# A hybrid decoder step on one core: projection stores on ScalarE's queue, the gate's low parts on GpSimd, constant products ahead of column sums

## The chip, the cores and the metric

The kernel runs on one core of a Trainium2 chip. The time is the device time in microseconds of one execution of the whole program; the profile is one such execution recorded by the hardware, on its own. TensorE (PE in the rows) makes the matrix products and writes to PSUM; VectorE (DVE), ScalarE (ACT) and GpSimd (POOL) do the rest on tiles of 128 partitions; SyncE (SP) issues most DMA transfers. Each engine works through its own instructions in order, and they wait for each other by semaphores.

## The reference, cut to what matters

One step of one layer of a decoder: 1024 prompt rows and 8 x 8 sample rows (1088 columns in the kernel, which works on the transposed activations), model width 1024.

```python
h = rms_norm(x, norm_mix_g)
proj = h @ w_in                       # 2*256 columns for a convolution branch, 3*768 for q, k, v
a = silu(layer_norm(depthwise_conv(a_val * sigmoid(a_gate)), ...))      # width 31
o = attend(q, k, v)                   # 12 heads of 64, three dilated windows, merged
x = x + concatenate([a, o]) @ w_out
h = rms_norm(x, norm_ffn_g)
g = depthwise_conv_valid(h @ w_ffn_gate)                                # width 3, 2816 channels
x = x + (silu(g) * (h @ w_ffn_up)) @ w_ffn_down
y = rms_norm(x, norm_final_g)
```

The outputs are y for prompt and sample, k and v for the caches, and the last rows of both convolutions. Everything is in float32.

## The kernel before

**Products in three parts.** A float32 product is made from two rounded parts of each operand: `hi` is the operand rounded to the type float32r (an ACT copy), `lo` is the remainder (operand minus `hi`, a subtraction on DVE or POOL). Three products (hi by hi, lo by hi, hi by lo) are added up in PSUM; lines 192 to 194 and 962 to 965 issue them. So each weight tile and each activation tile costs one ACT copy and one subtraction before TensorE can use it.

**Stages.** First the norm and the projections. `project(p)` (line 447) runs for six pairs of heads; each loads three weight tiles (q, k, v), makes the products, and DVE evicts them from PSUM into a tile `x`, 1088 columns wide, for each of the three (lines 469, 473). `prompt_part` (line 496) then splits q and k into high and low parts, and stores to memory what the attention will load again in another layout: the two parts of q into `dq` and of k into `dk` (line 505), k itself to its output (line 503), v to its output (line 507), and v transposed, by way of TensorE and two ACT copies, into `dv` (line 514). The first three projections go together with the sample rows' attention (`sample_attention`, cache tiles `cr`, line 176), the last three with the prompt's heads. `load_head` (line 617) loads `qs`, `kk`, `vf` and `vw` back. `scores` and `weighted` do the prompt's attention: masked scores on TensorE and DVE, exponentials on ACT (line 718), transposes on TensorE (line 745), their copies on ACT or DVE, and the products with v (line 766).

**The output projection** comes in three parts of 3, 3 and 2 tiles of 128 input channels (PARTS), because it starts before the last heads are done. The last part (from line 941) works on two halves of 544 columns. Its inputs and weights are loaded by a chain of loads on SP's queue (`queued`, `load_input`); `parts_of` (line 1011) splits a weight or an input, with ACT for the high part and POOL for the low part. Among the loads are the first tiles of the feed-forward gate, `gate_raw` (line 1067): four tiles 128x512, whose high parts ACT makes at line 1083 and whose low parts DVE makes at line 1084. The gate's first products (`two_products`, line 981, output px) read them.

`out_half(h, hook)` (line 1174) goes over the eight output tiles of a half in a fixed order. For each it makes the products into a pair of PSUM banks (`pair`, four pairs in rotation), DVE adds them to the residual (line 1188), ACT squares the sum (line 1197) and DVE adds up the squares (line 1201). In the second half the first three tiles also have a deferred product with the middle part's inputs; after that product of the second tile (j = 1) the hook `norm_first` (line 1214) puts the column sums of the first half's squares: `root` (line 207), five products with a column of ones (line 214), and a short chain on DVE and ACT that ends in the inverse root. `spread` (line 232) turns that into a row for all partitions, after j = 2.

**What sets the order.** A planner simulates the program and writes each engine's order by it; `tc.issue_after(x)` pins an instruction behind x, and where nothing pins it the planner chooses. DMA issues are instructions of the engine whose queue they are on, so a transfer that waits for its data holds up what stands behind it on that engine. `load_w` (line 155) already makes its low parts on POOL in pieces 256 wide (`cut`). `onesc` (line 141) is a constant 128x128 tile; a few products of it with itself stand at the kernel's start (line 296) and among its first products (line 362).

Of the kernel before, what the change touches and what calls it, by code (L numbers as in the profile page):

```python
# [18 lines left out]
F32 = mybir.dt.float32  # L19
# [5 lines left out]
P = 128  # L25
D = 1024
# [45 lines left out]
HF = NF // 2  # L72
BEHIND = 3
GS = (6, 7)
PO = 240
GW = 2 + S + B * (T + 2)
HALF = ((0, HN // 2), (HN // 2, HN // 2))
# [9 lines left out]
def trunk_kernel(tc, xT, w_in, w_first, w_out, w_gate, w_up, w_down, par, kc, vc, sa, sf, pmask, smask,  # L87
                 yT, kT, vT, ca, cas, cf):
    nc = tc.nc
    with (  # L90
# [50 lines left out]
        onesc = cp.tile([P, P], F32, name="onesc")  # L141
# [65 lines left out]
        def root(sq, div, width):  # L207


            ps = bank(*rbank[0])  # L210
            size = sizes(width)
            nt = len(size)
            for i, n in enumerate(size):
                summed[0] = nc.tensor.matmul(ps[:n, i:i + 1], sq[:, i * P:i * P + n], ones, start=True, stop=True).ins
            v = sp.tile([P, 9], F32, tag="rv", name=nm("rv"), bufs=2)[:, :nt]
            nc.vector.memset(v, 1.0)
            nf = width // P
            nc.vector.tensor_scalar(v[:, 0:nf], ps[:, 0:nf], 1.0 / div, EPS, op0=ALU.mult, op1=ALU.add)
            if nf < nt:
                n = size[-1]  # L220
                nc.vector.tensor_scalar(v[:n, nf:nt], ps[:n, nf:nt], 1.0 / div, EPS, op0=ALU.mult, op1=ALU.add)
            r = sp.tile([P, 9], F32, tag="rr", name=nm("rr"), bufs=2)[:, :nt]
            nc.vector.reciprocal(r, v)
            squared[0] = nc.scalar.activation(r, r, AF.Sqrt).ins

            t = sp.tile([P, 9], F32, tag="rt", name=nm("rt"), bufs=2)[:, :nt]
            nc.vector.tensor_mul(t, r, r)
            nc.vector.scalar_tensor_tensor(t, t, -0.5, v, op0=ALU.mult, op1=ALU.mult)
            rooted[0] = nc.vector.scalar_tensor_tensor(r, t, 1.5, r, op0=ALU.add, op1=ALU.mult).ins
            return r  # L230
# [63 lines left out]
        ps = bank("S", "g", 3)  # L294
# [152 lines left out]
        def project(p, pump):  # L447
            W = [load_w(w_in[4 + 6 * c + p], KT, nc.gpsimd, cut=2 * P) for c in range(3)]
            dq = dp.tile([2, P, S], F32, name=nm("dq"))
            dk = dp.tile([2, P, S], F32, name=nm("dk"))  # L450
            dv = dp.tile([S, P], F32, name=nm("dv"))
            if p < NS1:
                new, vn = zt("S", "new", 2, "new", 2 * NS), zt("S", "vn", 2, "vn", P)
            else:
                new, vn = zt("P", "new", NP - NS1, "new", 2 * NS), zt("P", "vn", NP - NS1, "vn", P)
            nc.gpsimd.memset(vn[NS:, :], 0.0)
            spill[p] = (dq, dk, dv), new, vn
            xs = {}

            evicted = [None]  # L460

            def product(c):
                if c not in xs:
                    xs[c] = keep("qkv")
                x = xs[c]

                def ev(ps, t0, n):
                    m = min(n, S - t0)
                    nc.vector.tensor_mul(by_class(x)[:, t0 // 4:(t0 + m) // 4, :],
                                         ps[:, :m].rearrange("p (j c) -> p j c", c=4),  # L470
                                         R[:, t0:t0 + m].rearrange("p (j c) -> p j c", c=4))
                    if m < n:
                        evicted[0] = nc.vector.tensor_mul(x[:, S:N], ps[:, m:n], R[:, S:N]).ins  # L473

                last = p == NP - 1 and c == 2
                gemm(W[c], h, KT, ev, ([("A", "g", GA)] * GA + [("A", "r", 1)]) if last else None)

            def split_qk(c, hi, lo, cols):
                x = xs[c][:, cols]
                if c == 0:  # L480
                    nc.scalar.activation(hi, x, AF.Copy, scale=-0.125)
                    nc.vector.scalar_tensor_tensor(lo, x, -0.125, hi.bitcast(F32), op0=ALU.mult, op1=ALU.subtract)
                else:
                    nc.scalar.activation(hi, x, AF.Copy)
                    nc.vector.tensor_sub(lo, x, hi.bitcast(F32))

            def sample_part(c):
                if c < 2:
                    nc.scalar.activation(new[:, c * NS:(c + 1) * NS], xs[c][:, S:N], AF.Copy,
                                         scale=(1.0 if c else -0.125))  # L490
                else:
                    pt = bank(*gbank[0])
                    nc.tensor.transpose(pt[:NS, :P], xs[c][:, S:N], ident)
                    nc.scalar.activation(vn[:NS, :], pt[:NS, :P], AF.Copy)

            def prompt_part(c):
                x = xs[c]
                if c < 2:
                    hi, lo = zbig("qkh", F32R, S), zbig("qkl", F32R, S)
                    split_qk(c, hi, lo, slice(0, S))  # L500
                if c < 2:
                    if c:
                        nc.sync.dma_start(kT[p * P:(p + 1) * P, :], x)
                    for part, t in ((0, hi), (1, lo)):
                        nc.sync.dma_start((dq, dk)[c][part], t.bitcast(F32))
                else:
                    nc.sync.dma_start(vT[p * P:(p + 1) * P, :], x)
                    vs = zbig("vs", F32, S)
                    for i0 in (0, 4):
                        pt = bank(*gbank[0])  # L510
                        for i in range(4):
                            nc.tensor.transpose(pt[:, i * P:(i + 1) * P], x[:, (i0 + i) * P:(i0 + i + 1) * P], ident)
                        nc.scalar.activation(vs[:, i0 * P:(i0 + 4) * P], pt, AF.Copy)
                    nc.sync.dma_start(dv.rearrange("(t p) d -> p t d", p=P), vs.rearrange("p (t d) -> p t d", d=P))

            for c in range(3):
                product(c)
                if c == 2 and p < NS1:
                    with tc.issue_after(evicted[0]):
                        pump(STEPS[c])  # L520
                else:
                    pump(STEPS[c])
                sample_part(c)
                prompt_part(c)
# [390 lines left out]
        part = load_part(PARTS[0], staged, g_part)  # L915
# [27 lines left out]
        def pair(s="g", tag="g2"):  # L943

            return zone[pairs[0] + "ps"].tile([P, 1024], F32, tag=tag, name=nm(s), bufs=pairs[1])
# [65 lines left out]
        def parts_of(raw, hi, lo):  # L1011

            done = nc.scalar.activation(hi, raw, AF.Copy).ins
            nc.gpsimd.tensor_sub(lo, raw, hi.bitcast(F32))
            return done

        part, late_lows = [[], []], []
# [25 lines left out]
        for h, tag in enumerate(("b11", "t2")):  # L1043
# [4 lines left out]
            for m0 in ORDER[h * 4:h * 4 + 4:2]:  # L1048
                raw = slot("b11", "wr", F32, 2 * n * P)
                queued(raw.rearrange("p (m c) -> p m c", m=2), w_out[m0:m0 + 2, :, k0 * P:].rearrange("m p c -> p m c"))  # L1050
                hi, lo = early["b21"].pop() if early["b21"] else slot("b21", "wh", w=512), slot("b21" if m0 == ORDER[0] else "t3", "wl", w=512)
                with tc.issue_after(last_high):
                    last_high = parts_of(raw, hi, lo)
                hi, lo = [t.rearrange("p (k c) -> p k c", c=P) for t in (hi, lo)]
                for j in range(2):
                    wl[m0 + j] = hi[:, j * n:j * n + n], lo[:, j * n:j * n + n]
        for i in range(n1):
            lo, hi = slot("b21", "ml"), slot("t3", "mh")
            raw = lo.bitcast(F32)
# [12 lines left out]
        for m in ORDER[:DEFER]:  # L1072
            hi, lo = [slot("b22", t, w=n1 * P) for t in ("wh", "wl")]
# [7 lines left out]
        for r, (hi, lo) in zip(gate_raw, tiles):  # L1081
            with tc.issue_after(last_high):
                last_high = nc.scalar.activation(hi, r, AF.Copy).ins
            nc.vector.tensor_sub(lo, r, hi.bitcast(F32))

        blocks = {tag: [None] * 4 for tag in BTAGS}
        made, high = [], [None]
# [77 lines left out]
        raw = [slot("t2", "wr", F32, half) for _ in range(4)]  # L1165
# [45 lines left out]
        sq0, _ = out_half(0, None)  # L1211
        rs = []

        def norm_first(j, last):
            if j == 1:
                with tc.issue_after(last):
                    rs.append(root(sq0, D, HN))
                order = squared[0]
                for x, (hi, lo) in up_parts:
                    with tc.issue_after(order):  # L1220
                        order = nc.scalar.activation(hi, x, AF.Copy).ins
                    with tc.issue_after(rooted[0]):
                        nc.vector.tensor_sub(lo, x, hi.bitcast(F32))
            elif j == 2:
                with tc.issue_after(last):
                    rs[0] = spread(rs[0], new_root, HN)
# [301 lines left out]
        w, act = [], []  # L1528
# [45 lines left out]
        for k, (g, unit) in enumerate(UNITS):  # L1574
# [16 lines left out]
            for i, product in enumerate(unit):  # L1591
                b, key, outs = product
                for m in range(4):
# [6 lines left out]
                    for r, h in outs:  # L1600
                        x = x2[4 * r + m][:, h * HN:h * HN + HN]
# [67 lines left out]
        for i, (t0, n) in enumerate(TAIL):  # L1669
            r = []  # L1670
# [20 lines left out]
        v, r, t = [sp.tile([P, 9], F32, tag=tag, name=nm(tag), bufs=2)[:, :nt] for tag in ("rv", "rr", "rt")]  # L1691
# [118 lines left out]
```

## Time and profile before

| | us |
|---|---|
| median of 3 runs | 1316.93 |
| lowest and highest | 1312.14, 1317.67 |
| the profiled execution | 1320.17 |
| its span, first to last instruction | 1318.4 |
| mean granted TensorE clock | 0.993 of full |
| TensorE busy | 1293.7 |
| VectorE busy | 932.1 |
| ScalarE busy | 561.2 |
| GpSimd busy | 503.0 |

Rows of the profile are quoted below word for word. In a group's row stand line, engine, operation, output<-inputs and count, then busy time and mean; in a row of time, start and length in us come first and the idle time before, with what ended it, last in brackets. In a row of waits stand the engine and line that waited, what it waited for, and total us, count and longest. In a row of windows stand the stretch, its length, and busy us (with the number of instructions) of PE, PE's weight loads, DVE, ACT and POOL, then the granted TensorE clock, the mean busy share of the 16 DMA engines, and GB/s. "SPq" is SP's instruction queue. A matmul's length in a row includes the time through the array; successive starts show the pace.

### The profile page before, as it was taken

What the parts mean: (1) busy time and instruction counts of PE and PEld (TensorE: products, weight loads), DVE (VectorE), ACT (ScalarE), POOL (GpSimd) and SP (SyncE); (2) the same over time, 40 slices, a digit from 0 to 9 for tenths busy, and PEclk for the clock granted to TensorE, in tenths of its full rate; (3) what the DMA queues carried; (4) which work ended last, traced back from release to release, by engine and by line L of the source; (5) the groups of instructions that cost most, each with busy time, mean ns of one, the idle gap of its engine ahead of it and who ended that gap; (6) DMA issues with size and microseconds to landing.
All of it is one profiled execution on the core that took longest, in us unless ns stands there. A gap on an engine that the chain in (4) does not pass through costs nothing.

```text
span 1318.4 us, 26089 instructions
## 1 busy us (share of the span) xinstructions
PE 1293.7 (98%) x10336; PEld 1252.6 (95%) x10336; DVE 932.1 (71%) x1788; ACT 561.2 (43%) x1124; POOL 503.0 (38%) x475
## 2 busy tenths in 40 slices
PE   9999999999999999899999999999999999999997
PEld 8999999999978889899999999999999999999997
DVE  7478879555674657589976767667776569868656
ACT  7312121547684564455433323333233344334523
POOL 0242223211111117321765645656465535444611
PEclk9999999999999999999999999999999999999998
DMA  9248778565789987360213323133312395352413
GB/s 320 65 151 294 270 255 217 158 174 139 235 271 293 289 272 207 102 228 18 75 50 124 124 92 110 47 124 109 108 65 91 113 358 188 109 185 90 158 36 102
DMA packets 93530, 211.43 MB, mean 160 GB/s; under 512 B 13792, under 2 KB 42592, under 8 KB 93408
## 3 DMA queue, kind: packets, MB, share of 16 engines
q1 hardware_dynamic: 92688, 208.89, 48.2%
q8 instruction: 81, 1.33, 0.4%
q10 hardware_dynamic: 720, 0.88, 0.2%
q14 instruction: 41, 0.34, 0.1%
HBM read 153.69 MB, written 56.04 MB: 159 GB/s over the span
## 4 chain that ended last, share of the span: by engine, by line
PE 79%; DVE 12%; DMA 5%; issue 2%; ACT 1%; SPq 0%; POOL 0%; DVEq 0%; ACTq 0%
PE g L192 6%; PE g L193 6%; PE g L194 6%; PE py L962 5%; PE py L964 5%; PE py L965 4%; PE g L962 4%; PE g L965 4%; PE g L964 4%; PE pz L964 3%; PE pz L965 3%; PE pz L962 3%; PE o L766 3%; PE px L962 3%; PE px L965 3%; PE px L964 3%
## 5 line engine op out<-in xcount | busy, mean ns | idle before, releaser
L167 POOL TENSOR_TENSOR wl<-wr,wh 128x256 fp32r<-128x256 f32 x96 | 85.3, 918 | 253.6 <-PE g L194 111.0
L192 PE MATMUL g<-xh,wh 128*128 128x384 f32 (+1 forms) x472 | 156.9, 332 | 0.3 <-DVE qkv L473 0.2
L194 PE MATMUL g<-xh,wl 128*128 128x384 f32 (+1 forms) x472 | 155.5, 330 | 0.0
L193 PE MATMUL g<-xl,wh 128*128 128x384 f32 (+1 forms) x472 | 155.1, 329 | 0.0
L962 PE MATMUL g<-ux,as 128*128 128x272 f32 x504 | 145.1, 288 | 0.4 <-DVE x L1602 0.4
L965 PE MATMUL g<-ux,as 128*128 128x272 f32 x504 | 145.3, 288 | 0.0
L964 PE MATMUL g<-ux,as 128*128 128x272 f32 x504 | 144.7, 287 | 0.0
L1116 POOL TENSOR_TENSOR wb<-wr,wb 128x512 fp32r<-128x512 f32 x79 | 115.6, 1475 | 50.7 <-ACT wb L1115 50.7
L1512 POOL TENSOR_TENSOR as<-ar,as 128x640 fp32r<-128x640 f32 (+1 forms) x56 | 90.4, 1625 | 103.2 <-ACT as L1511 91.4
L1115 ACT ACTIVATE wb<-wr 128x512 fp32r<-128x512 f32 x79 | 49.7, 629 | 163.5 <-DVE wr L1150 104.3
L1116 POOL TENSOR_TENSOR wa<-wr,wa 128x512 fp32r<-128x512 f32 x40 | 63.7, 1593 | 91.3 <-ACT wa L1115 85.3
L962 PEld LDWEIGHTS g<-ux,as 128*128 128x128 f32 x504 | 95.0, 189 | 0.8 <-issue 0.8
L718 ACT ACTIVATE y<-y,m 128x128 f32<-128x128 f32 (+1 forms) x192 | 88.5, 463 | 16.6 <-DVE m L706 13.1
L965 PEld LDWEIGHTS g<-ux,as 128*128 128x128 f32 x504 | 94.8, 188 | 0.0
L964 PEld LDWEIGHTS g<-ux,as 128*128 128x128 f32 x504 | 94.6, 188 | 0.0
L1380 DVE SCALAR_TENSOR_TENSOR fc<-gb,prm,fc 128x1104 f32<-128x1104 f32 x44 | 82.0, 1885 | 14.7 <-ACT fc L1378 14.4
L192 PEld LDWEIGHTS g<-xh,wh 128*128 128x128 f32 x472 | 88.7, 188 | 2.1 <-issue 0.6
L193 PEld LDWEIGHTS g<-xl,wh 128*128 128x128 f32 x472 | 88.8, 188 | 0.3
L194 PEld LDWEIGHTS g<-xh,wl 128*128 128x128 f32 x472 | 88.8, 188 | 0.0
L681 DVE CUSTOM_DVE_ANT_0 y<-s,pmk 128x128 f32<-128x128 f32 (+1 forms) x192 | 63.6, 376 | 27.6 <-PE s L677 25.4
L419 DVE SCALAR_TENSOR_TENSOR cacc<-gp,prm,cacc 128x1024 f32<-128x1024 f32 x60 | 79.8, 1329 | 0.1
L163 ACT ACTIVATE wh<-wr 128x1024 fp32r<-128x1024 f32 (+1 forms) x28 | 28.0, 999 | 111.5 <-PE g L194 93.2
(413 smaller groups left out, 4309.2 us busy)
## 6 DMA issues: line engine op xcount, KB each, us to landing
cr<-in_kc SPq DMA_DIRECT2D x24, 768.0 KB, 8.5
cr<-in_vc SPq DMA_DIRECT2D x24, 768.0 KB, 7.7
ux<-ub SPq DMA_DIRECT2D x63, 272.0 KB, 4.1
kk<-dk SPq DMA_DIRECT2D x48, 256.0 KB, 6.2
wr<-in_w_in SPq DMA_DIRECT2D x20, 512.0 KB, 5.2
wr<-in_w_gate SPq DMA_DIRECT2D x20, 512.0 KB, 3.2
wr<-in_w_up SPq DMA_DIRECT2D x20, 512.0 KB, 4.5
ub<-u SPq DMA_DIRECT2D x18, 544.0 KB, 3.4
```

The lines of the kernel that those rows point to most:

```text
L167: lo_eng.tensor_sub(lo[:, t], raw[:, t], hi.bitcast(F32)[:, t])
L192: nc.tensor.matmul(ps[c], whi[:, k, :], xh[:, t0:t0 + n], start=(k == 0), stop=False)
L193: nc.tensor.matmul(ps[c], whi[:, k, :], xl[:, t0:t0 + n], start=False, stop=False)
L194: nc.tensor.matmul(ps[c], wlo[:, k, :], xh[:, t0:t0 + n], start=False, stop=(k == nk - 1))
L419: eng.scalar_tensor_tensor(acc[:, :S], gp[:, j:j + S], col(w0 + j), acc[:, :S], op0=ALU.mult, op1=ALU.add)
L718: nc.scalar.activation(y, y, AF.Exp, bias=m[:, 4 * g + i:4 * g + i + 1], scale=-1.0, accum_out=den[:, g, 2 * hd + u, i:i + 1])
L962: nc.tensor.matmul(ps, whi[:, k, :], xh[:, t], start=(start and k == 0), stop=False, skip_group_check=True)
L964: nc.tensor.matmul(ps, whi[:, k, :], xl[:, t], start=False, stop=False, skip_group_check=True)
L965: last = nc.tensor.matmul(ps, wlo[:, k, :], xh[:, t], start=False, stop=(stop and k == nk - 1), skip_group_check=True).ins
L1116: nc.gpsimd.tensor_sub(lo, x, hi.bitcast(F32))
L1380: nc.vector.scalar_tensor_tensor(c[:, :W], gb[i][:, t:t + W], col(C_FW + 3 * f + t), c[:, :W], op0=ALU.mult, op1=ALU.add)
L1512: nc.gpsimd.tensor_sub(lo, raw, hi.bitcast(F32))
```

## The change

Three edits. In `prompt_part` the stores of k's output, of both high parts, of v's output and of `dv` are issued from ACT's queue; the low parts stay on SP's. In the output projection's last part the subtractions of `parts_of` are cut into two halves of the width, and the gate's low parts go from DVE to POOL, also in two halves. In `norm_first` three products of `onesc` with itself, into a pair of PSUM banks of their own whose content nothing reads, are put between the deferred product of j = 1 and the column sums, which are pinned behind them.

```diff
+BRIDGE = 3
...
                 if c < 2:
                     if c:
-                        nc.sync.dma_start(kT[p * P:(p + 1) * P, :], x)
-                    for part, t in ((0, hi), (1, lo)):
-                        nc.sync.dma_start((dq, dk)[c][part], t.bitcast(F32))
+                        nc.scalar.dma_start(kT[p * P:(p + 1) * P, :], x)
+                    for part, t, store in ((0, hi, nc.scalar.dma_start), (1, lo, nc.sync.dma_start)):
+                        store((dq, dk)[c][part], t.bitcast(F32))
                 else:
-                    nc.sync.dma_start(vT[p * P:(p + 1) * P, :], x)
+                    nc.scalar.dma_start(vT[p * P:(p + 1) * P, :], x)
...
-                    nc.sync.dma_start(dv.rearrange("(t p) d -> p t d", p=P), vs.rearrange("p (t d) -> p t d", d=P))
+                    nc.scalar.dma_start(dv.rearrange("(t p) d -> p t d", p=P), vs.rearrange("p (t d) -> p t d", d=P))
...
         def parts_of(raw, hi, lo):
 
             done = nc.scalar.activation(hi, raw, AF.Copy).ins
-            nc.gpsimd.tensor_sub(lo, raw, hi.bitcast(F32))
+            w = raw.shape[-1] // 2
+            for t in (slice(0, w), slice(w, 2 * w)):
+                nc.gpsimd.tensor_sub(lo[:, t], raw[:, t], hi.bitcast(F32)[:, t])
             return done
...
                 last_high = nc.scalar.activation(hi, r, AF.Copy).ins
-            nc.vector.tensor_sub(lo, r, hi.bitcast(F32))
+            for t in (slice(0, D // 4), slice(D // 4, D // 2)):
+                nc.gpsimd.tensor_sub(lo[:, t], r[:, t], hi.bitcast(F32)[:, t])
...
             if j == 1:
                 with tc.issue_after(last):
+                    ps = pair()
+                    for _ in range(BRIDGE):
+                        end = nc.tensor.matmul(ps[:, :P], onesc, onesc, start=True, stop=True).ins
+                with tc.issue_after(end):
                     rs.append(root(sq0, D, HN))
```

## The prediction

> **What bounds the kernel now.** I read the page's head first, then the waits of TensorE, then the windows of 20 us, and last the order of time around the two places that the change touches.
>
> ```profile
> span 1318.4 us, 26089 instructions
> PE 1293.7 (98%) x10336; PEld 1252.6 (95%) x10336; DVE 932.1 (71%) x1788; ACT 561.2 (43%) x1124; POOL 503.0 (38%) x475
> PE o L766 <- DMA vw<-dv: 2.9, 1, 2.9
> PE g L214 <- DVE sq L1201: 1.0, 1, 1.0
> 380.00:400.00 20.00, 18.34 (x146) 14.23 (x144) 15.42 (x51) 14.54 (x45) 0.87 (x1) 1.00 1.03 348
> 400.00:420.00 20.00, 17.14 (x143) 16.00 (x145) 9.63 (x41) 9.46 (x27) 2.44 (x5) 0.91 0.97 285
> 580.00:600.00 20.00, 19.91 (x153) 19.48 (x153) 19.00 (x31) 11.64 (x21) 0.00 (x0) 0.98 0.26 99
> ```
>
> The reader sees that TensorE (PE) sets the end: it stands idle for 1318.4 - 1293.7 = 24.7 us of the whole span, 1.9%. No change that leaves the products alone can win more than that and the stretches at a lower granted clock (the third column from the right, 0.91 and 0.98 above). Two idle places belong to this change. One is a wait for the load of vw at about 408 to 411 us, behind the projections. The other is a wait of the column sums (L214) for the running sum of squares, in the output projection's last part. I take the second first, since it can be worked out.
>
> **The output projection's last part.** These are VectorE's (DVE) and TensorE's rows in order of time, with two of GpSimd's (POOL).
>
> ```profile
> 559.29 4.02 POOL L1014 TENSOR_TENSOR ml<-ml,mh 128x544 fp32r<-128x544 f32 x3
> 566.21 4.14 POOL L1014 TENSOR_TENSOR wl<-wr,wh 128x384 fp32r<-128x384 f32 x3 [2.90 <-DMA wr<-in_w_up]
> ...
> 562.78 1.11 DVE L1201 TENSOR_TENSOR sq<-sq,sq 128x544 f32<-128x544 f32 x1
> 569.40 1.55 DVE L1201 TENSOR_TENSOR sq<-sq,sq 128x544 f32<-128x544 f32 x1
> 570.86 0.71 DVE L1188 TENSOR_TENSOR x<-g,x 128x544 f32<-128x544 f32 x1
> 571.50 0.71 DVE L1201 TENSOR_TENSOR sq<-sq,sq 128x544 f32<-128x544 f32 x1
> 572.13 1.28 DVE L1084 TENSOR_TENSOR wa<-wr,wa 128x512 fp32r<-128x512 f32 x2
> 573.33 1.28 DVE L1084 TENSOR_TENSOR wb<-wr,wb 128x512 fp32r<-128x512 f32 x2
> 574.54 0.71 DVE L1201 TENSOR_TENSOR sq<-sq,sq 128x544 f32<-128x544 f32 x1
> 575.17 0.71 DVE L1188 TENSOR_TENSOR x<-g,x 128x544 f32<-128x544 f32 x1
> 575.81 0.71 DVE L1201 TENSOR_TENSOR sq<-sq,sq 128x544 f32<-128x544 f32 x1
> ...
> 575.39 0.28 PE L965 MATMUL g<-mh,wl 128*128 128x272 f32 x1
> 576.66 1.22 PE L214 MATMUL g<-ones,sq 128*128 128x1 f32 x10 [0.99 <-DVE sq L1201]
> 577.82 0.59 PE L962 MATMUL g<-mh,wh 128*128 128x272 f32 x1
> 580.93 0.32 PE L964 MATMUL g<-ml,wh 128*128 128x272 f32 x1
> ```
>
> The four subtractions of L1084 (the gate's low parts) hold VectorE from 572.13 to 574.54, 2.4 us, ahead of the last two additions of squares. TensorE ends its products at 575.39 + 0.28 = 575.67 and waits 0.99 us. What follows is slower too: 13 products start between 577.82 and 580.93, 0.239 us apart.
>
> ```profile
> 578.00:578.50 0.50, 0.50 (x3) 0.50 (x4) 0.33 (x3) 0.10 (x1) 0.00 (x0) 0.50 0.15 57
> 574.13 0.29 PE L964 MATMUL g<-ml,wh 128*128 128x272 f32 x1
> ```
>
> The granted clock is 0.50 there. At the full clock ten such products lie between 574.13 and 575.39, 0.126 us apart, so the 13 would take 1.64 us and not 3.11: 1.47 us lost. The place costs 0.99 + 1.47 = 2.46 us.
>
> What the change puts there. The subtractions become eight on GpSimd, half as wide (128x256). The nearest rows for one, and for one constant product of the bridge (two records each), are these:
>
> ```profile
> L167 POOL TENSOR_TENSOR wl<-wr,wh x96: 723/739/1854, 46.3 to 536.2; 128x256 fp32r<-128x256 f32 x96
> L362 PEld LDWEIGHTS g<-onesc x6: 188/192/192, 5.7 to 6.4; 128*128 128x128 f32 x6
> ```
>
> Eight by 0.74 is 5.9 us of GpSimd after 570.35, to 576.3, or some 577.5 with the halved L1014 before them and VectorE's operations in between. Nothing wants them before the gate's first product:
>
> ```profile
> 591.73 0.13 PE px L983
> ```
>
> That is 14 us later, so the work is hidden; without this cover its cost would be at most those 5.9 us.
>
> But GpSimd's work holds up VectorE's additions. The one at 562.78 ended at 563.89, 0.58 after GpSimd's run ended (559.29 + 4.02 = 563.31). The one at 569.40 ended at 570.95, 0.60 after GpSimd's end at 570.35. So an addition of two SBUF tiles seems to wait out the GpSimd operation under way; the additions from PSUM (L1188) keep their 0.71. With the subtractions gone, VectorE needs four steps (three L1201, one L1188) from 571.50, 0.63 apart, so it is done at 574.0; with a whole 0.74 of waiting before each of the three, at 576.2. The bridge is six records some (6.4 - 5.7)/5 = 0.14 us apart, 0.84 us: TensorE is through it at 575.67 + 0.84 = 576.51. Both ends of VectorE's range lie before that. The sums then start at 576.51 and not 576.66: 0.15 us won, and if TensorE isn't idle the 1.47 us of half clock go as well. The term is **-1.6 us**; its ends are -2.5 (no bridge cost at all) and +0.84 (bridge paid, nothing won). After that the same chain runs on behind TensorE's order, so what is won is kept: VectorE, 19.00 of 20 us busy from 580 to 600, starts that stretch from the root that these sums feed.
>
> The Trainium skill ("TensorE: Matmul & The Clock Gate", Part 1) says that the clock falls after an idle window of about 3.4 us, and that the windows run freely. This trace shows the fall after 0.99 us of waiting and 1.2 us of one-column sums, so the idle need not last a window. By the rule the half clock would stay where the windows happen to lie badly, and the term would be -0.15 us.
>
> The halves of parts_of. Each halved operation costs GpSimd 2 x 0.74 in place of one 128x512 row.
>
> ```profile
> 554.30 5.04 POOL L1014 TENSOR_TENSOR wl<-wr,wh 128x512 fp32r<-128x512 f32 x4
> L896 POOL TENSOR_TENSOR x<-x,xr x32: 752/769/1040, 500.4 to 528.7; 128x272 f32<-128x272 f32 x32
> 555.84 0.36 PE L962 MATMUL g<-mh,wh 128*128 128x272 f32 x1 [0.75 <-DVE x L900]
> ```
>
> 5.04/4 = 1.26 becomes 1.48; 4.02/3 = 1.34 becomes 2 x 0.77 = 1.54; the 128x384 stay between 1.38 and 1.48. The first seven add 1.5 us, inside the 2.90 us that GpSimd waits before 566.21. The first of the last three would end by 567.7, where TensorE (96 products from 555.84 at 0.126) wants it near 568. I take +0.1 us, ends 0 and +0.6.
>
> **The projections' stores.** Per projection seven stores; five (k's output, both high parts, v's output, dv) go to ScalarE's (ACT) queue, 30 in all, and the two low parts stay. These are SyncE's queue (SP) waits from 60 to 365 us, then its order behind the last projection:
>
> ```profile
> SPq L507 <- DVE qkv L473: 31.9, 5, 8.5
> SPq L503 <- DVE qkv L473: 29.7, 5, 11.9
> PE ss L596 <- DMA cr<-in_vc: 0.8, 2, 0.4
> PE s L677 <- DMA qs<-dq: 0.6, 1, 0.6
> ...
> 370.28 0.34 SPq L507 DMA_DIRECT2D out_vT<-qkv  x1
> 373.39 0.54 SPq L159 DMA_DIRECT2D wr<-in_w_out  x1
> 376.06 0.38 SPq L514 DMA_DIRECT2D dv<-vs  x1
> 376.49 2.26 SPq L281 DMA_DIRECT2D mx<-mixed  x3
> SPq L176 <- PE t L745: 2.3, 1, 2.3
> ```
>
> The long waits of the queue before 365 us cost TensorE almost nothing: the loads behind them make it wait 0.8 + 0.6 us. Behind the last projection dv holds the queue from 373.93 to 376.49, 2.56 us, and the loads of mx, of the caches, of qs, kk, vf and vw follow in order. Without it they could go up to 2.5 us earlier. Two things take from that: the queue's own 2.3 us wait for TensorE among the cache loads, and the DMA engines, which are full (shares 1.03 and 0.97 in the first windows). So vw lands between 0 and 2.5 us earlier, out of the 2.9 us wait. I take 1.0, nearer to the low end because of the full engines; no clock is counted.
>
> ScalarE pays 30 x 0.34 = 10.2 us for issuing, the length of the L507 row. Most lies in its idle time (43% busy). Behind a store that waits on VectorE stand the exponentials (L718), the copies of the transposed weights (L751) and the weights' high parts (L163), and TensorE's transposes and products wait for those. SyncE's queue loses the 30 issues; GpSimd's issues nothing. Ends: 0, and 10.2 if each stood on the path; I take +0.3.
>
> **Sum.** -1.6 + 0.1 - 1.0 + 0.3 = -2.2 us. The profiled execution took 1320.17 us, 1.8 around its span, so it would become 1318.0. The median of the runs is 1316.93, 3.2 lower; the same difference gives **1314.7 us**.
>
> **Rivals.**
> 1. The vw wait goes wholly, with its half clock: the 2.9, some 1.7 lost to the 0.91 (0.09 x 20), the 1.4 of the other loads, and the 1.6 above, less 0.4: 7.2 us, 1309.7. For it: the queue waits are long. Against it: full DMA engines.
> 2. The stores' move does nothing, because the same bytes go through the same full engines. Then -1.6 + 0.1 + 0.3 = -1.2: 1315.7. For it speak shares of 1.03 and 0.97 just ahead of the vw wait. The Trainium skill ("DMA: Bandwidth & Descriptors", Issuing engines are not separate DMA queues) says the same: only issue time is saved.
> 3. The bridge is not covered, or the planner puts the sums ahead of the second product's rest, before VectorE is ready: TensorE still waits and the clock still falls. Up to 0.84 is paid and nothing won there: 0.84 + 0.1 - 1.0 + 0.3 = +0.2, 1317.2.
> 4. Slower: ScalarE stands at the stores. In SyncE's queue the same stores stood up to 11.9 us. If ScalarE's order puts one ahead of exponentials whose transposes TensorE wants, TensorE waits and falls to half clock. At some 3 us and 1.5 us of clock a time, two of the six projections give +9 beside the -1.6 + 0.1 of the other part: 1324.4. It decides from the point where the store's wait exceeds the slack of the exponentials, which are at most 0.7 us late now.
>
> ```profile
> PE t L745 <- ACT y L718: 1.1, 2, 0.7
> ```
>
> **How the numbers follow.** Chances: forecast 0.42, rival 1 0.14, rival 2 0.22, rival 3 0.14, rival 4 0.08. The order that the planner writes may also shift elsewhere by a microsecond or two either way; so rivals 2 and 3 and the forecast are read with some 2 us around them. The range 1307.5 to 1321 takes in all but rival 4 and the far end of rival 1. A change under 0.5% (6.6 us) is about what can't be told from none here: below 1310.3 lies most of rival 1 and a little of the forecast, 0.15; above 1323.5 rival 4, 0.08; between, 0.77.
>
> **What would show it.** Right: L214 in that part without a wait, granted clock 1.00 from 576 to 581, the gate's low parts on GpSimd before 580; the vw wait near 2 us. Wrong: a half clock still there; L745 or L766 waiting on ScalarE by more than now; cache loads later, not earlier. A change of TensorE's order in the projections would make the sum void.

## The result, and the profile after

| | before | after |
|---|---|---|
| median, us | 1315.46 (4 runs) | 1337.52 (4 runs) |
| lowest to highest | 1312.14 to 1317.67 | 1336.06 to 1338.52 |
| the profiled execution | 1320.17 | 1336.72 |
| its span | 1318.4 | 1334.9 |

The changed kernel takes 1.0146 times as long, with an interval of 1.0111 to 1.018. The forecast was 1314.7 us and the range ended at 1321.0. Run again later, beside other experiments (e8 below), it took 1.0088 times as long, 1.0059 to 1.0116: slower both times, but not by the same amount.

These are TensorE's longest waits in the changed kernel (total us, count, longest). Numbers of lines after 74 are higher by 1, by up to 4 in the last part.

```profile
PE s L678 <- DMA qs<-dq: 5.2, 2, 4.1
PE o L767 <- DMA vw<-dv: 4.1, 1, 4.1
PE s L656 <- DVE xe L653: 4.1, 3, 3.4
```

The wait for vw was to become shorter than its 2.9 us; it is 4.1, and the one for qs stands above it. The wait of the column sums is gone from the list. Where the time went is seen by following three marks that both kernels have: the last copy of vs behind the projections, the first product of the output projection's last part (555.84 before) and the end. First the copy in the kernel before, then both marks in the changed one:

```profile
375.44 0.60 ACT L513 ACTIVATE vs<-g 128x512 f32<-128x512 f32 x1 [0.69 <-PE g L512]
```

```profile
379.23 0.60 ACT L514 ACTIVATE vs<-g 128x512 f32<-128x512 f32 x1 [0.73 <-PE g L513]
573.23 0.36 PE L963 MATMUL g<-mh,wh 128*128 128x272 f32 x1 [0.75 <-DVE x L901]
```

Up to the copy 379.23 - 375.44 = 3.8 us are lost, between the marks 194.0 - 180.4 = 13.6, and behind the second mark 762.6 - 761.7 = 0.9 are won: together the 16.5 us of the two spans. (Most of the first 3.8 can also stand in a kernel that moves no store: in e11 below the copy starts at 378.29.) So the loss lies among the prompt's heads, and the windows there show how it looks, before and after:

```profile
400.00:420.00 20.00, 17.14 (x143) 16.00 (x145) 9.63 (x41) 9.46 (x27) 2.44 (x5) 0.91 0.97 285
480.00:500.00 20.00, 19.81 (x205) 17.19 (x199) 15.38 (x61) 15.86 (x45) 3.18 (x4) 1.00 0.62 214
540.00:560.00 20.00, 17.73 (x142) 16.85 (x141) 9.17 (x16) 10.33 (x19) 8.56 (x8) 1.00 0.31 100
```

```profile
400.00:420.00 20.00, 14.43 (x109) 12.39 (x107) 8.99 (x40) 7.62 (x23) 3.17 (x4) 0.93 1.07 260
480.00:500.00 20.00, 15.87 (x119) 14.15 (x118) 7.91 (x40) 8.84 (x27) 1.04 (x1) 0.83 0.85 251
540.00:560.00 20.00, 15.06 (x108) 13.41 (x106) 13.08 (x24) 7.62 (x23) 8.01 (x12) 0.83 0.21 64
```

The reader sees three separate holes and not one: TensorE's busy time (third number) falls by 2.7, 3.9 and 2.7 us, and in the last two the granted clock (third column from the right) falls as well. Two things limit this view. The changed kernel is by then 4 to 17 us behind, so a window doesn't hold quite the same work in both; and the holes aren't the same in every execution. In e8, the same kernel again, the stretch between the marks took 185.1 us in place of 194.0, TensorE waits 0.7 us for qs in place of 5.2, and the second window looks like this:

```profile
480.00:500.00 20.00, 19.27 (x179) 16.86 (x182) 10.75 (x50) 11.80 (x39) 1.04 (x1) 1.00 0.77 238
```

The first hole starts at the store that was moved. In the kernel before, dv was issued at 376.06, as soon as its copy was done, ahead of the loads of mx and of the caches. Its time from issue to landing there, then in the changed kernel:

```profile
DMA to landing us min/median/max: 5.5/5.5/5.5
```

```profile
L515 ACTq DMA_DIRECT2D dv<-vs x1: 378/378/378, 381.4 to 381.4; - x1
...
DMA to landing us min/median/max: 13.4/13.4/13.4
```

And SyncE's queue in the changed kernel, in order of time, with its wait:

```profile
377.65 2.62 SPq L282 DMA_DIRECT2D mx<-mixed  x3
...
382.75 12.44 SPq L177 DMA_DIRECT2D cr<-in_kc  x3
395.28 1.09 SPq L623 DMA_DIRECT2D qs<-dq  x2
```

```profile
SPq L177 <- DMA dv<-vs: 10.7, 1, 10.7
```

The three loads of mx now go ahead of dv, and two cache loads are issued on SyncE's queue within 2.5 us behind it, at 382.7 and 383.8; dv lands at 381.4 + 13.4 = 394.8. The third cache load goes into the place in SBUF that vs leaves, so it waits for that landing, and qs, kk, vf and vw stand behind it: qs is issued at 395.28 and not at 383.77. Up to 392 us the DMA engines stay as full as before (shares of 1.03 to 1.05); in the last part of the wait they run dry; before and after:

```profile
392.00:396.00 4.00, 3.96 (x36) 2.98 (x25) 2.61 (x7) 2.42 (x10) 0.00 (x0) 1.00 1.05 248
```

```profile
392.00:396.00 4.00, 4.00 (x34) 3.79 (x31) 3.74 (x7) 3.63 (x11) 0.00 (x0) 1.00 0.49 153
```

This reading explains the first hole. Whether it explains the loss is what the experiments are about.

In the last part the wait is gone. TensorE's, VectorE's and GpSimd's rows in the changed kernel:

```profile
591.76 0.83 PE L1223 MATMUL g<-onesc 128*128 128x128 f32 x6
592.35 0.37 PE L963 MATMUL g<-mh,wh 128*128 128x272 f32 x1
593.94 1.10 PE L215 MATMUL g<-ones,sq 128*128 128x1 f32 x10
...
592.40 0.71 DVE L1205 TENSOR_TENSOR sq<-sq,sq 128x544 f32<-128x544 f32 x1
...
571.75 5.60 POOL L1017 TENSOR_TENSOR wl<-wr,wh 128x256 fp32r<-128x256 f32 x8
585.24 4.85 POOL L1017 TENSOR_TENSOR wl<-wr,wh 128x192 fp32r<-128x192 f32 x6 [3.50 <-ACT wh L1014]
590.05 4.35 POOL L1088 TENSOR_TENSOR wa<-wr,wa 128x256 fp32r<-128x256 f32 x4
594.37 2.81 POOL L1088 TENSOR_TENSOR wb<-wr,wb 128x256 fp32r<-128x256 f32 x4
```

```profile
595.00:599.00 4.00, 4.00 (x34) 4.00 (x33) 3.55 (x10) 2.53 (x6) 2.18 (x4) 1.00 0.28 109
```

No wait stands in the row of the sums, and the four us behind them run at the full clock. The constant products cost TensorE 592.35 - 591.76 = 0.59 us. They don't stand right ahead of the sums, though: the planner put twelve of the part's own products between them (592.35 to 593.94). VectorE's last addition ends at 592.40 + 0.71 = 593.11, when the constant products are over, so it is the twelve that cover the rest.

### The profile page after: what moved, and what is told of

Read it like the earlier page. It is cut to its first block, busy times and chain, and to the rows that moved or that the text cites. A ratio compares the mean times of both kernels' runs of the same rounds, so it can differ in the third digit from the quotient of the medians.

```text
span 1334.9 us, 26079 instructions
## 1 busy us (share of the span) xinstructions
PE 1300.6 (97%) x10342; PEld 1257.6 (94%) x10342; DVE 925.7 (69%) x1784; ACT 562.0 (42%) x1124; POOL 514.3 (39%) x493
## 4 chain that ended last, share of the span: by engine, by line
PE 71%; DVE 12%; DMA 8%; ACT 3%; POOL 3%; issue 2%; SPq 0%; DVEq 0%; ACTq 0%; POOLq 0%
PE g L193 5%; PE g L195 5%; PE g L194 5%; PE py L963 4%; PE py L966 4%; PE py L965 4%; PE g L963 3%; PE g L966 3%; PE g L965 3%; PE px L963 3%; PE px L966 3%; PE px L965 3%; PE pz L965 3%; PE pz L963 3%; PE pz L966 3%; PE s L678 2%
## 5 line engine op out<-in xcount | busy, mean ns | idle before, releaser
L1610 DVE TENSOR_TENSOR x<-g,x 128x544 f32<-128x544 f32 x76 | 52.5, 715 | 35.0 <-PE g L966 34.7
```

## The experiments

Each time is a ratio to the kernel before, run on the same chip, with its 95% interval.

**First: which part.** e1 has the last part alone (all stores on `nc.sync`), e2 the stores alone.

> Only the output projection's last part as changed (gate's low parts and the halves on GpSimd, three constant products); all projection stores on SyncE's queue. Theory A (the loss comes from the projections' stores alone): 1312 to 1316 us, about 1.5 us under before, and the 0.5 clock behind the column sums is gone. Rival B (the last part loses too): 1318 us or more. If A is right, the waits for qs and vw stay as in before (at most 3 us each).

Measured: 0.9989 [0.9974, 1.0005], 1316.4 us.

> Only the stores moved (k's and v's outputs, high parts, dv: 30 on ScalarE's queue); the last part as before. Theory A: 1335 to 1341 us, all of the loss. Rival B: under 1328 us.

Measured: 1.0098 [1.0066, 1.013], 1330.9 us. That lies between the two expectations; but the changed kernel itself took 1329.3 us on this chip (e8), so the stores carry the whole loss.

**Second: which stores.** e3 moves 24 of the 30 and leaves dv, e4 moves only dv's six.

```diff
-                    for part, t, store in ((0, hi, nc.sync.dma_start), (1, lo, nc.sync.dma_start)):
+                    for part, t, store in ((0, hi, nc.scalar.dma_start), (1, lo, nc.sync.dma_start)):
...
-                    nc.sync.dma_start(dv.rearrange(...
+                    nc.scalar.dma_start(dv.rearrange(...
```

> As e2, but dv's stores back on SyncE's queue; 24 stores on ScalarE's. Theory A1 (dv is what costs: on ScalarE's queue it is issued behind the exponentials, lands late, and the cache loads that wait for it, 10.7 us in the changed kernel, hold the queue): 1313 to 1320 us. Rival A2 (the planner's new order of TensorE's products, about as far changed by any of the moves, is what costs): 1323 us or more. Rival A3 (30 issues' time on ScalarE): loss in proportion to the count, 24/30 of e2's, about 1333 us.

Measured: 1.0019 [0.9994, 1.0044].

> Only dv's six stores on ScalarE's queue, the other 24 on SyncE's, last part as before. Theory A1: 1328 us or more. Rival A2: 1318 to 1330 us, no more than e3. Rival A3: 6/30 of e2's loss, about 1320 us.

Measured: 1.0067 [1.0039, 1.0095], 1326.9 us, a little less than theory A1 had. So dv is enough for most of it, and the number of issues doesn't set the loss: six cost no less than 24.

**Third: which dv, and what waits for it.** e5 is the changed kernel with the last projection's dv back in SyncE's queue, e6 the kernel before with only that one moved, e7 the changed kernel with a place of its own for the last vs, and e8 the changed kernel unaltered.

```diff
-                    nc.scalar.dma_start(dv.rearrange(...
+                    (nc.sync if p == NP - 1 else nc.scalar).dma_start(dv.rearrange(...
...
-                    vs = zbig("vs", F32, S)
+                    vs = keep("vs", S) if p == NP - 1 else zbig("vs", F32, S)
```

> The changed kernel with one store of the 30 back on SyncE's queue: dv of the last projection. Theory C (the whole loss hangs on this one store: on ScalarE's queue it goes behind the loads of mx and of the first cache tile, lands after 11 to 13 us and not 6, and the next cache load, whose place is the one that vs leaves, holds SyncE's queue for some 10 us): within 3 us of before, no wait of L177 for dv over 3 us. Rival D (each projection's dv costs its share): 5/6 of the loss stays, ratio 1.012.

Measured: 1.0011 [0.9995, 1.0027].

> The kernel before with one store moved to ScalarE's queue: dv of the last projection. Theory C: about e4's ratio, 1.006 to 1.010 (+8 to +13 us), with L177 waiting some 10 us for dv. Rival D: a sixth of it, 1.001.

Measured: 1.005 [1.0016, 1.0084].

> The changed kernel, dv's last store still on ScalarE's queue, but its source vs in a tile of the pool of long-lived tiles, so that the cache loads that come next don't take its place and don't wait for the store. Theory C (the wait, not the late landing itself, is the cost): within 4 us of before, no wait of L177 for dv. Rival E (the store's late landing or the planner's order costs without the wait): still 1.01 or more.

Measured: 1.0018 [0.9993, 1.0044].

> The changed kernel unaltered, beside the others on the same chip. Theory C and rivals: 1.012 to 1.017 of before. If it is nearer 1.010, its distance from e2 (1.0098) lay in the chips, and the two edits add up.

Measured: 1.0088 [1.0059, 1.0116]. SyncE's wait for dv in e6, then in e7, and dv's time to land in e7:

```profile
SPq L177 <- DMA dv<-vs: 9.7, 1, 9.7
```

```profile
SPq L638 <- DMA dv<-vs: 5.7, 1, 5.7
```

```profile
DMA to landing us min/median/max: 18.4/18.4/18.4
```

One store out of 30 decides, the last dv. In e7 it lands later than ever, but only the load of vw waits for it, and the loss is not clear of nothing. At this point the wait at the cache load looked like the whole cause.

**Fourth: two kernels that the wait doesn't explain.** e9 is the last part with all stores in SyncE's queue and the last vs in its own place. e10 is the changed kernel with the last dv issued under `tc.high_priority`, ahead of some of ScalarE's exponentials. e11 and e12 are the last part without and with the constant products.

```diff
-                    nc.scalar.dma_start(dv.rearrange(...
+                    with tc.high_priority(offset=AHEAD) if p == NP - 1 else nullcontext():
+                        nc.scalar.dma_start(dv.rearrange(...
...
-                    ps = pair()
-                    for _ in range(BRIDGE):
-                        end = nc.tensor.matmul(ps[:, :P], onesc, onesc, start=True, stop=True).ins
+                    end = last
```

> All projection stores in SyncE's queue as before, the output projection's last part changed, and the last projection's vs in a place of its own, which the next cache load doesn't take. Theory (a load that waits for dv to land holds SyncE's queue; in the kernel before by 1.9 us): that 1.9 us goes from the queue, the loads of kk, qs and vw go up to 1.9 us earlier, and the last part brings its 1.4 us: 2 to 4 us under the kernel before, ratio 0.997 to 0.999. Rival (an own place moves the order elsewhere and the queue's next wait takes over): as the last part alone, 0.999 or over.

Measured: 1.0064 [1.004, 1.0087], with these two rows (wait, landing):

```profile
SPq L631 <- DMA dv<-vs: 0.9, 1, 0.9
```

```profile
DMA to landing us min/median/max: 11.9/11.9/11.9
```

> The changed kernel, but the last projection's dv store stands some instructions earlier in ScalarE's order. Theory C1 (dv lands late because ScalarE issues it late, behind exponentials): issued within 0.5 us of the end of its copy, it lands in about 6 us, SyncE waits for it under 4 us, ratio at or under 1.003. Theory C2 (it lands late because mx and the cache loads, no longer behind it in one queue, share the DMA engines with it): still 9 us or more to land, SyncE waits 7 us or more, ratio 1.005 or over.

Measured: 1.0026 [1.0006, 1.0046], with these:

```profile
SPq L177 <- DMA dv<-vs: 10.5, 1, 10.5
```

```profile
DMA to landing us min/median/max: 15.6/15.6/15.6
```

In e10 dv was issued at 380.6, as its copy ended (380.01 + 0.60), and still took 15.6 us: so ScalarE's issuing it late is not why it lands late. What is left is the traffic it shares the DMA engines with: the first two loads of mx had been issued, the third and the cache loads followed. But the wait of 10.5 us cost 0.26% here against 0.88% in e8, and e9 lost 0.64% with a wait of 0.9 us; there the planner, freed of the shared place, put mx's loads and three cache loads ahead of dv in the same queue. A cause that is there with little of the loss, and a loss nearly without the cause: the wait is not all of it. What else differs is the order that the planner writes for every engine behind 390 us.

> The last part changed with all projection stores in SyncE's queue, but without the six constant products ahead of the column sums. Prediction's step: VectorE is done with its additions between 574.0 and 576.2 on the clock of the kernel before, TensorE at 575.7, so without the bridge the sums wait between 0 and 0.5 us; if 0, the time is up to 0.8 us under that with the bridge and no half clock stands behind the sums. Rival (the bridge is what keeps the clock): a wait of over 0.3 us at the sums, granted clock 0.50 for some 3 us, 1.5 us more than with the bridge.

Measured: 0.9972 [0.9952, 0.9992].

> The last part changed alone, all stores in SyncE's queue, as in the first experiment, so that the two above stand beside it on one chip: 0.9985 to 0.9995 of the kernel before if the prediction's -1.6 + 0.1 us holds; 1.0000 or over if that gain was noise.

Measured: 1.0004 [0.9988, 1.002], which by the expectation speaks for noise. TensorE's and VectorE's rows of e11:

```profile
581.69 0.28 PE L966 MATMUL g<-mh,wl 128*128 128x272 f32 x1
581.98 1.18 PE L215 MATMUL g<-ones,sq 128*128 128x1 f32 x10
```

```profile
578.21 2.35 DVE L1205 TENSOR_TENSOR sq<-sq,sq 128x544 f32<-128x544 f32 x2
581.13 0.71 DVE L1205 TENSOR_TENSOR sq<-sq,sq 128x544 f32<-128x544 f32 x1
```

VectorE is done at 581.84, TensorE's products at 581.97. The sums come without a wait and without the constant products, by 0.13 us.

**Fifth: queue and order crossed.** At the end of the trace each engine's instructions, except the moved stores, are chained in the order read from the finished program of another kernel. e13 has the 30 stores on ScalarE's queue and the order of the kernel before; e14 has them in SyncE's queue and the order of e2; e15 is e2 again; e16 has only the last dv moved, in the old order; e17 has 24 stores moved without dv, in the old order.

```diff
-        trunk_kernel(tc, *args)
+        trunk_kernel(tc, *args); pin_order(tc, nc)
+# pin_order, for each engine, along the other kernel's order:
+    tc.add_manual_dep(i, prev.name, mybir.DependencyInfo(mybir.DependencyClass.NoSync, mybir.DependencyReason.DATA), reason="order")
```

> The stores alone, as in the second experiment, but on every engine all other instructions stand in exactly the order of the kernel before, so only the 30 stores differ. Theory H (the wait itself: dv lands late, the next cache load stands in SyncE's queue for it, and the loads behind it come late for TensorE): SyncE waits some 10 us for dv, TensorE waits for qs, kk or vw, ratio 1.006 to 1.010 as with the planner's own order. Theory O (the planner, told of another queue, writes a worse order, and the wait alone costs little): ratio 0.999 to 1.002. Between: both have a part.

Measured: 1.0029 [1.0007, 1.005].

> The other half of the cross: all stores in SyncE's queue as in the kernel before, everything else on every engine in exactly the order that the planner wrote for the stores alone. Theory H: dv lands in about 6 us, SyncE waits for it 2 us, ratio 0.999 to 1.002. Theory O: ratio 1.006 to 1.010 though dv lands early.

Measured: 1.0071 [1.0043, 1.0098].

> The stores alone once more, in the planner's own order, on the same chip as the two crossed kernels, so that the three stand beside one another: 1.007 to 1.012 if the second experiment's 1.0098 [1.0066, 1.013] holds here. The sum of what the two crossed kernels lose should come near it if queue and order add up.

Measured: 1.0134 [1.0104, 1.0163].

> The kernel before with one store, dv of the last projection, on ScalarE's queue, and all else on every engine in exactly the old order. Theory H: SyncE waits 9 to 10 us for dv, ratio about as in the sixth experiment, 1.004 to 1.008. Theory O: the same wait, but the ratio at 0.999 to 1.002.

Measured: 1.0031 [1.0007, 1.0056].

> 24 of the 30 stores on ScalarE's queue, dv's six in SyncE's, all else on every engine in exactly the order of the kernel before. If the queue's share of the loss (0.29% for 30 stores, 0.31% for the last dv alone) is all dv's, and the prediction's rival 2 holds for the other stores: ratio 0.999 to 1.001, SyncE waits for dv 2 us. If leaving SyncE's queue wins what the prediction gave it (1.0 us, up to 2.5): 0.998 to 0.9995. If ScalarE pays for the issues: over 1.001.

Measured: 0.9994 [0.997, 1.0018].

| | old order | new order |
|---|---|---|
| stores in SyncE's queue | 1 (before) | 1.0071 (e14) |
| stores in ScalarE's queue | 1.0029 (e13) | 1.0134 (e15) |

Neither theory is the whole: the queue alone costs 0.29%, the order alone 0.71%, both 1.34%, 0.34% more than the sum, which the intervals allow for. In microseconds of 1318 these are 3.8, 9.4 and 17.7. The queue's part seems to be that of the last dv (e16 0.31%; e17, without it, nothing that is clear, though its interval overlaps the others). In the traces of e13, e16 and e17 every engine's sequence, the moved stores left out, is that of the kernel before, and in e14 that of e2; and since e17 takes no longer than the kernel before, the chaining itself costs nothing that can be seen.

The same comparison of sequences settles e10. Its engines follow the order of e5 but for a few exchanged neighbours, while e8 has the order of e2 (the last part and two exchanges behind it aside). So e10 is e5's order with the late dv, 1.0026 against 1.0011, a step that e13's interval (0.07 to 0.5%) allows; and e10 and e8 have the same late dv but different orders. e3 has e5's order too: not every new order costs as much as e2's.

The waits show queue and order apart. e16 has SyncE's long wait, and TensorE waits for loads behind it:

```profile
SPq L177 <- DMA dv<-vs: 9.6, 1, 9.6
```

```profile
PE o L767 <- DMA vw<-dv: 3.6, 1, 3.6
PE ss L571 <- DMA cr<-in_kc: 2.1, 1, 2.1
```

In e13 the queue stands as long:

```profile
SPq L177 <- DVE ml L285: 9.6, 1, 9.6
```

The row names VectorE, but dv, issued at 380.6, lands after 11.9 us, at 392.5, and the wait ends at 392.6. Where TensorE loses the 0.3% is not shown by the profiles. In e13 its wait for vw is 1.1 us, shorter than before; and from the last copy of vs to the first product of the last part e13 took 179.4 us and e16 180.1, against 180.4 in the kernel before and 176.3 in e17, each in one execution.

In e14 SyncE waits 1.5 us for dv. But in the new order TensorE meets loads of qs that haven't landed (twice), and a slow stretch near the end of the heads:

```profile
430.99 1.08 PE L677 MATMUL s<-kk,qs 128*128 128x128 f32 x8 [2.23 <-DMA qs<-dq]
485.51 1.09 PE L677 MATMUL s<-kk,qs 128*128 128x128 f32 x8 [1.12 <-DMA qs<-dq]
```

```profile
540.00:560.00 20.00, 16.82 (x117) 13.86 (x116) 8.86 (x20) 9.10 (x25) 1.51 (x2) 0.83 0.07 26
```

The ten loads of qs between 375 and 575 us land after 8.7 us in the median; in the kernel before after 4.2. First e14, then before:

```profile
DMA to landing us min/median/max: 3.5/8.7/11.9
```

```profile
DMA to landing us min/median/max: 3.4/4.2/14.7
```

In e15, with both, the waits for vw and for qs stand together, with one for VectorE:

```profile
PE o L767 <- DMA vw<-dv: 5.6, 1, 5.6
PE s L678 <- DMA qs<-dq: 5.5, 3, 3.3
PE s L656 <- DVE xe L653: 4.1, 3, 3.7
```

This is an execution of 1339.6 us; in that of e2, the same kernel at 1323.2 us, the waits for vw and qs were 3.6 and 2.6. Why the planner's new order is the slower one is argued from these rows and not tested apart.

**Last: what beats both.** e18 is e11 on another chip.

> The last part changed without the constant products, all stores in SyncE's queue, once more on another chip. In the eleventh experiment the sums came without a wait at the full clock, so the constant products only cost their 0.6 us: 0.996 to 0.999 of the kernel before if that run's 0.9972 [0.9952, 0.9992] holds, 0.9995 or over if it was chance.

Measured: 0.9973 [0.9949, 0.9996]. Twice 0.27 to 0.28% faster than the kernel before, 1315.1 and 1315.3 us against 1317.8 and 1318.7: all stores in SyncE's queue, the gate's low parts and the halves on GpSimd, and no constant products. That these products are what keeps e12 from it is not shown: on the trace they are 0.59 us, 0.04%.

## Why the prediction was wrong, step by step

**What bounds the kernel: right.** TensorE sets the end, and the loss appears as its waits and half clock.

**The projections' stores: the step that failed**, in two places. The first is "Without it they could go up to 2.5 us earlier." It took the store out of SyncE's queue and left out what its place there was good for. The loads of mx, which used to stand behind it, are now issued before it, those of the cache soon after on the other queue. They share the DMA engines with it, and it lands after 10.9 to 15.6 us on ScalarE's queue in the kernels where a cache load waits for it, and not after 5.5; and that load, taking vs's place, stops the queue for some 10 us. The dependence could be read from the kernel before, in a row that the prediction did not use:

```profile
SPq L176 <- DMA dv<-vs: 1.9, 1, 1.9
```

The prediction listed "full DMA engines" as a reason for a small gain, where they were the reason for a loss. With the order held, the term is not -1.0 but +3.8 us (e13, interval 0.9 to 6.6). The other 24 stores gave nothing clear (e17, from -4.0 to +2.4 us), as rival 2 had it. The Trainium skill's rule that was cited for that rival ("DMA: Bandwidth & Descriptors", Issuing engines are not separate DMA queues) agrees with e17. For dv the new queue changes what goes ahead of it, and that costs time.

The second is the sentence that the planner's order "may also shift elsewhere by a microsecond or two either way". On its own the shift costs 0.71%, 9.4 us (e14), more than any term of the sum. The last line of the prediction, that a change of TensorE's order would make the sum void, was the right warning, but it stood there without a price: the range was drawn as if the order stayed.

**ScalarE's issuing, +0.3: neither shown nor refuted.** e17 moves 24 issues to it, and its interval is too wide to tell 0.3 us from nothing. Rival 4 had the right sign (1324.4) by the wrong mechanism: in the changed kernel TensorE's long waits are for loads and VectorE, not for the exponentials.

**The last part, -1.6 and +0.1: right in its mechanism, not clear in size.** e1 and e12 give 0.9989 and 1.0004, that is -1.4 and +0.5 us with some 2 us on either side. Behind the mark at 573.23 the changed kernel won 0.9 us. With the subtractions gone from VectorE the sums come without a wait in all profiles of the changed last part but one (e9 waits 0.39 us), and the clock stays at 1.00 behind them in all. The constant products, priced at 0.84, cost 0.59; by e11 they weren't needed, since the subtractions' leaving was enough. So rival 3 is out in the changed kernel. The halves on GpSimd took 5.60/8 = 0.70 us each, as priced, and the narrow ones of 192 columns 4.85/6 = 0.81, more than the 0.74 that a 128x256 was given (rows of GpSimd above).

The 1.47 us of half clock, counted as certain, are likely and not certain: the same wait is not always followed by it. Eight profiles have a wait of 0.98 us or more there; the clock falls to 0.50 within 2 us behind it in six (before, e6, e14 to e17) and stays at 1.00 in two (e2, e3). In e3 and e17 the last part is as before, and the sums wait as long; first e3, then e17, each with the two us behind the sums:

```profile
575.10 1.18 PE L215 MATMUL g<-ones,sq 128*128 128x1 f32 x10 [0.99 <-DVE sq L1205]
```

```profile
576.10:578.10 2.00, 2.00 (x18) 1.99 (x18) 1.41 (x7) 1.32 (x4) 0.00 (x0) 1.00 0.02 6
```

```profile
573.76 1.18 PE L215 MATMUL g<-ones,sq 128*128 128x1 f32 x10 [0.98 <-DVE sq L1205]
```

```profile
575.76:577.76 2.00, 2.00 (x11) 2.00 (x11) 1.93 (x7) 2.00 (x5) 0.00 (x0) 0.50 0.01 4
```

The clock is 1.00 behind a wait of 0.99 us, 0.50 behind one of 0.98. The prediction set the Trainium skill's freely running windows ("TensorE: Matmul & The Clock Gate", Part 1) against one profile. The pair of profiles is in keeping with windows that run freely, though no run here shows the windows themselves. That the idle must last a whole window of 3.4 us doesn't agree with e17, where the clock fell after 0.98 us of waiting and the one-column sums.

## What to carry to other kernels

A store's place in a queue is also its place ahead of the loads behind it: before moving one, ask what will overtake it on the DMA engines and which load waits for its source's place. Where a planner writes the order, an edit is priced twice, once with the order held and once with the new one, and the second can be the larger; pinning every engine to the other kernel's order tells the two apart. One profile shows that a wait is there, but not that the half clock behind it comes every time. And ask of a row of waits not only how long it is now but what it waits for: 1.9 us for dv became 10 once dv landed late.

## What was not expected of the hardware

- Near the end of the 10.7 us for which SyncE's queue stood, from 392 to 396 us, the DMA engines' share was 0.49, where it had been 1.05: engines that had been full up to then ran dry.
- The same store of dv took 5.4 to 6.2 us to land where the loads of mx and of the cache tiles stood behind it in the queue, and 10.9 to 18.4 us where two or all three of mx's loads were issued first (e9, in SyncE's queue too: 11.9).
- A wait of about 1 us on TensorE was followed by half clock in one execution and not in another (0.50 in e17, 1.00 in e3; it came in six of eight profiles).
